# First norm of a decoder layer on one Trainium2 core: fp16 halves split in token layout and turned by DMA transposes

## The chip, the cores and the metric

The kernel runs on one NeuronCore of a Trainium2 chip. The metric is the device time in microseconds (us) of one execution. Engines are named as in the profile: PE is TensorE (PEld its weight loads), DVE is VectorE, ACT is ScalarE, POOL is GpSimd, SP is SyncE, which here only issues DMAs. A name with a q, such as SPq, is the queue of that engine's instructions.

## The reference

One decoder layer over 1024 tokens of 1024 columns, in float32. Cut to what matters:

```python
h = rms_norm(x, norm_mix_pre)                 # x * rsqrt(mean(x*x) + 1e-6) * gain
proj = h @ w_in                               # q, k, v, three conv inputs, two gates
o = stick_breaking_attention(q, k, v)         # 8 heads of 64, strictly causal
m = sigmoid(g_att) * (o @ w_att) + sigmoid(g_conv) * ((cb * causal_dwconv(cc * cx)) @ w_conv)
x = x + rms_norm(m @ w_out, norm_mix_post)
u = causal_dwconv(rms_norm(x, norm_ffn_pre) @ w_up)      # 2 * 2816 columns
a, g = split(u)
x = x + rms_norm((gelu(g) * a) @ w_down, norm_ffn_post)
```

## The kernel before

Every float32 matrix product is made of three fp16 products: an operand is scaled by a power of two and split into a high half (the value rounded to fp16) and a low half (the rest), and high x high, high x low and low x high are summed in PSUM (`PASSES`). The high half is written by an ACT activation, the low half by a DVE `scalar_tensor_tensor`.

This case is about the first stage of `mixer`: the first RMS norm, and the turn of the normed x into `hT`. `hT` is one buffer of shape [128, 2, 8, 1024]: columns of h on the partitions, two halves, eight blocks of 128 columns, 1024 tokens. All products that read h take it from there: the v product has it as the stationary operand (L343, L371), q, k, the conv inputs and the gates as the moving one (L200).

x comes as eight tiles of 128 tokens by 1024 columns, one 512 KB DMA each (`load_x`, L307). The steps of tile tt are small helpers: `square_x` (ACT, sum of squares, L56), `rstd_x` (a DVE step at L170, then a power on POOL at L171), `norm_x` (DVE, times the root and the gain row `gb`, in place, L317), `turn_x` (eight TensorE transposes of float32 blocks into PSUM, L322), `high` (ACT, PSUM to the high half of `hT`, L325), `low` (DVE, PSUM to the low half of `hT`, L328). `gain_max` and `gain_pow2` (DVE, L176 to L186) find the power of two for the halves of h, `s_h`, from the gain row; `high` and `low` use it.

Beside these run the weights of v, four tiles `st[0..3]`: their sums of squares (`sumsq` on ACT for tiles 0, 1, 3; a DVE instruction, `jk_v_2`, L424, for tile 2), their common scale `s_v` (`scale_of`: a few small DVE steps around one tiny matmul with a matrix of ones, L74), their high halves `w_high` (ACT, L375) and low halves `w_low` (DVE, L378). `v_pass(tt, ...)` is a group of v matmuls of token tile tt (L371). `square_w` fetches the raw tile of the next weights (q, then k; DMA at L383) and takes its sum of squares; `open_w` makes its scale (again with a tiny matmul, L74) and its high half (L392), and the function that it returns makes the low half (L396). `v_out` evicts one tile of v (ACT L333, DVE L335). `qk_tile` is a product of q or k, 24 matmuls for each half of the tokens (L200).

The order of this stage is written out by hand: within `tc.manual_schedule(engines={PE, DVE, Activation})` each of these three engines gets its instructions in the order of the program text. SP's queue is not in that set, so that a scheduler places the DMA issues. In the trace each engine starts its instructions in the order of its queue, so one that waits holds up those behind it on its engine. From `v_tile` of tile 4 and the attention on, the order is again the scheduler's.

Of the kernel before, what the change touches and what calls it, by code (L numbers as in the profile page):

```python
# [16 lines left out]
F16 = mybir.dt.float16  # L17
BF16 = mybir.dt.bfloat16
F32 = mybir.dt.float32
I32 = mybir.dt.int32  # L20
AF = mybir.ActivationFunctionType
ALU = mybir.AluOpType
AX = mybir.AxisListType

P = 128
T = 1024
D = 1024
KD = D // P
# [9 lines left out]
class Layer:  # L38
# [225 lines left out]
    def mixer(self, mid):  # L264
        tc, nc, a = self.tc, self.nc, self.a
        hT = self.hp.tile([P, 2, KD, T], F16, tag="hT", name="hT")
        with ExitStack() as ph1:
# [30 lines left out]
                yield  # L298


            with tc.tile_pool(name="ptp", bufs=2, space=bass.MemoryType.PSUM) as ptp:
                gb = self.slot([P, D], F32, "g_pre")
                xt, rt, pt = {}, {}, {}

                def load_x(tt):
                    xt[tt] = self.slot([P, D], F32, f"x{tt}")
                    nc.sync.dma_start(xt[tt], a["x"][ds(tt * P, P), :])  # L307

                def square_x(tt):
                    rt[tt] = self.small(f"r_pre{tt}")  # L310
                    self.sumsq(xt[tt], rt[tt][:, 0:1], f"n_pre{tt}")

                def rstd_x(tt):
                    rt[tt] = self.rstd(rt[tt])

                def norm_x(tt):
                    nc.vector.scalar_tensor_tensor(xt[tt], xt[tt], rt[tt], gb, ALU.mult, ALU.mult)  # L317

                def turn_x(tt):
                    pt[tt] = ptp.tile([P, KD, P], F32, tag="pt", name=f"pt_pre{tt}")  # L320
                    for k in range(KD):
                        nc.tensor.transpose(pt[tt][:, k, :], xt[tt][:, ds(k * P, P)], self.ident)  # L322

                def high(tt):
                    nc.scalar.activation(hT[:, 0, :, ds(tt * P, P)], pt[tt], AF.Copy, scale=s_h)  # L325

                def low(tt):
                    nc.vector.scalar_tensor_tensor(hT[:, 1, :, ds(tt * P, P)], pt[tt], s_h,  # L328
                                                   hT[:, 0, :, ds(tt * P, P)], ALU.mult, ALU.subtract)

                def v_out(tt, pv):
                    pj = pv.rearrange("p (j two d) -> p j two d", two=2, d=64)
                    nc.scalar.activation(v16[tt // 2][:, tt % 2, :, 0:4:3, :], pj, AF.Copy, scale=2.0 ** -15)  # L333
                    for e in range(2):
                        nc.vector.scalar_tensor_tensor(v16[tt // 2][:, tt % 2, :, 1 + e, :], pj[:, :, e, :], 2.0 ** -15,  # L335
                                                       v16[tt // 2][:, tt % 2, :, 3 * e, :], ALU.mult, ALU.subtract)
# [18 lines left out]
                    if i == 0:  # L355
                        load_x(1)
                load_x(2)
                load_x(3)
                nc.sync.dma_start(self.cmw, a["conv_mix"])
                nc.sync.dma_start(self.cfw, a["conv_ffn"])  # L360
                wv = [self.wh.tile([P, 2, D], F16, tag="wh", name=f"wh_v_{i}") for i in range(4)]
                sm_v = self.small("sm_v")
                ET = mybir.EngineType
                pv = [None] * 4

                def v_pass(tt, ks, passes, first=False, last=False):
                    if first:
                        pv[tt] = pm.tile([P, NH], F32, tag="pm", name=f"pv{tt}")
                    todo = [(k, p) for k in ks for p in passes]
                    for n, (k, (hi, wi)) in enumerate(todo):  # L370
                        nc.tensor.matmul(pv[tt], hT[:, hi, k, ds(tt * P, P)], wv[k // 2][:, wi, ds((k % 2) * NH, NH)],  # L371
                                         start=first and n == 0, stop=last and n == len(todo) - 1)
# [4 lines left out]
                def w_low(i):  # L377
                    nc.vector.scalar_tensor_tensor(wv[i][:, 1, :], st[i], s_v, wv[i][:, 0, :], ALU.mult, ALU.subtract)  # L378
# [20 lines left out]
                def square_w(n, which):  # L399
                    raw[which] = fetch(n)  # L400
                    sm0[which] = self.small(f"sm_{which}0")
                    self.sumsq(raw[which], sm0[which][:, 0:1], f"{which}0_0")
# [2 lines left out]
                    for _ in range(n):  # L405
                        next(gen)

                for tt in range(4, 8):
                    load_x(tt)
                with tc.manual_schedule(engines={ET.PE, ET.DVE, ET.Activation}):  # L410
                    square_x(0)
                    rstd_x(0)
                    norm_x(0)
                    turn_x(0)
                    g_sm = self.gain_max(gb, "pre")
                    self.sumsq(st[0], sm_v[:, 0:1], "v_0")
                    square_x(1)
                    s_h, inv_h = self.gain_pow2(g_sm, 2)
                    self.sumsq(st[1], sm_v[:, 1:2], "v_1")
                    rstd_x(1)  # L420
                    norm_x(1)
                    turn_x(1)
                    high(0)
                    nc.vector.scalar_tensor_tensor(self.slot([P, D], F32, "jk_v_2"), st[2], 1.0, st[2], ALU.mult, ALU.mult,  # L424
                                                   accum_out=sm_v[:, 2:3])
                    self.sumsq(st[3], sm_v[:, 3:4], "v_3")
                    high(1)
                    s_v, inv_wv = self.scale_of(sm_v, 4, keep=True)
                    low(0)
                    low(1)  # L430
                    for i in range(4):
                        w_high(i)
                        if i == 2:
                            square_x(2)
                        for tt in range(2):
                            v_pass(tt, (2 * i, 2 * i + 1), ((0, 0), (1, 0)), first=i == 0)
                    w_low(0)
                    rstd_x(2)
                    w_low(1)
                    norm_x(2)  # L440
                    v_pass(0, range(0, 4), ((0, 1),))
                    turn_x(2)
                    square_x(3)
                    rstd_x(3)
                    w_low(2)
                    w_low(3)
                    v_pass(0, range(4, 8), ((0, 1),), last=True)
                    square_x(4)
                    norm_x(3)
                    high(2)  # L450
                    rstd_x(4)
                    square_w(1, "q")
                    low(2)
                    v_pass(1, range(8), ((0, 1),), last=True)
                    turn_x(3)
                    norm_x(4)
                    v_out(0, pv[0])
                    square_w(2, "k")
                    lq = open_w(1, "q")
                    high(3)  # L460
                    low(3)
                    v_out(1, pv[1])
                    square_x(5)
                    v_pass(2, range(8), PASSES, first=True, last=True)
                    rstd_x(5)
                    turn_x(4)
                    lq()
                    lk = open_w(2, "k")
                    norm_x(5)
                    high(4)  # L470
                    v_out(2, pv[2])
                    lk()
                    low(4)
                    square_x(6)
                    rstd_x(6)
                    v_pass(3, range(8), PASSES, first=True, last=True)
                    turn_x(5)
                    high(5)
                    norm_x(6)
                    v_out(3, pv[3])  # L480
                    low(5)
                    self.wdone["v"] = wv, inv_wv
                    self.wpos = self.fpos = 3
                    cst = self.small("cst", keep=True)

                    nc.vector.tensor_scalar(cst[:, 0:1], inv_h, inv_h, 2.0 ** 27, ALU.mult, ALU.mult)
                    nc.vector.tensor_scalar(cst[:, 1:2], inv_h, inv_wv, 2.0 ** 15, ALU.mult, ALU.mult)
                    inv_ov = cst[:, 1:2]
                    gens0 = [qk_tile(0, "q"), qk_tile(0, "k")]
                    run(gens0[0], 8)  # L490
                    square_x(7)
                    rstd_x(7)
                    turn_x(6)
                    high(6)
                    norm_x(7)
                    low(6)
                    self.fetch_to(4)
                    run(gens0[1], 8)
                    turn_x(7)
                    high(7)  # L500
                    low(7)


            pat = pha.enter_context(tc.tile_pool(name="pat", bufs=1, space=bass.MemoryType.PSUM))
# [781 lines left out]
```

## Time and profile before

| | |
|---|---|
| time, median of 3 runs | 1368.22 us (1367.43 to 1368.27) |
| profiled execution, first to last instruction (span) | 1365.7 us; no other time is given for this execution |
| PE busy | 1336.1 us, 98% of the span |
| DVE busy | 1028.6 us, 75% |
| ACT busy | 860.7 us, 63% |
| DMA | 96.06 MB, mean 70 GB/s |
| mean granted TensorE clock | 0.998 |

The profile was taken of one execution. Its page gives the busy time of each engine, the span in 40 slices of 34 us, the DMA queues, and the costliest groups of instructions. The first slice holds the stage of this case. In a row of the timeline the columns are start, duration, engine, line, operation, output and inputs, count, and in brackets the idle time before it with the instruction that ended it; several like instructions in a row are merged and have a count.

### The profile page before, as it was taken

How to read it: one execution, taken by the hardware profiler on the slowest of the kernel's cores; microseconds unless marked ns; L12 is line 12 of the kernel's file. 1: busy time of each engine (PE TensorE's matmuls, PEld its weight loads, DVE VectorE, ACT ScalarE, POOL GpSimd, SP SyncE). 2: the span in 40 equal slices, each digit the busy share in tenths (PEclk: the TensorE clock that was granted, in tenths of full speed). 3: DMA queues.
4: the chain of work that ended last, by engine and by line, in shares of the span. 5: the costliest groups of instructions: out<-in, count | busy, mean ns of one | idle time of the engine just before them, and what ended most of it. 6: DMA issues, size and time to landing. Idle time of an engine off the chain costs nothing. (4 is left out here: it accounts for less than half of the span.)

```text
span 1365.7 us, 16990 instructions
## 1 busy us (share of the span) xinstructions
PE 1336.1 (98%) x6651; PEld 607.7 (44%) x6651; DVE 1028.6 (75%) x1610; ACT 860.7 (63%) x1204; POOL 34.2 (3%) x52
## 2 busy tenths in 40 slices
PE   6999999999999999999999999999999999999997
PEld 3444444444444444444454444444444444444443
DVE  6667777777775965878788985984894896699855
ACT  6668778787775775666466577652761673476524
POOL 2000000000000000000010000000000000000002
PEclk9999999999999999999999999999999999999999
DMA  7102111101111121351331123122220321313216
GB/s 264 62 1 62 32 31 32 38 25 39 40 31 47 32 62 31 93 185 36 119 124 62 62 62 123 39 87 85 70 78 16 123 62 62 109 45 124 63 46 109
DMA packets 26576, 96.06 MB, mean 70 GB/s; under 512 B 3072, under 2 KB 3200, under 8 KB 26496
## 3 DMA queue, kind: packets, MB, share of 16 engines
q1 hardware_dynamic: 25056, 89.74, 20.3%
q0 software_dynamic: 1440, 5.24, 2.1%
q8 instruction: 52, 0.85, 0.2%
q14 instruction: 28, 0.23, 0.1%
HBM read 86.58 MB, written 8.39 MB: 70 GB/s over the span
## 5 line engine op out<-in xcount | busy, mean ns | idle before, releaser
L1156 PEld LDWEIGHTS <-wh_u 128*128 128x128 f16 x1848 | 178.8, 98 | 217.3 <-issue 3.5
L1048 PE MATMUL pd<-wdh,f 128*128 128x512 f16 (+1 forms) x1068 | 230.3, 377 | 2.8 <-ACT wdh L86 1.2
L1048 PEld LDWEIGHTS <-f 128*128 128x128 f16 x1068 | 104.4, 98 | 127.2 <-issue 4.3
L86 ACT ACTIVATE wh_u<-ws_u,sc 128x1024 f16<-128x1024 f32 (+1 forms) x66 | 64.7, 998 | 102.9 <-DVE sc L78 79.3
L1055 DVE SCALAR_TENSOR_TENSOR yacc<-pd,sd,yacc 128x512 f32<-128x512 f32 (+1 forms) x81 | 58.5, 740 | 72.7 <-PE pd L1048 65.2
L1156 PEld LDWEIGHTS <-wh_g 128*128 128x128 f16 x588 | 56.9, 98 | 68.7 <-issue 0.4
L859 PE MATMUL py<-wh_wo,m 128*128 128x512 f16 x384 | 83.9, 379 | 0.0
L87 DVE SCALAR_TENSOR_TENSOR wh_u<-ws_u,sc,wh_u 128x1024 f16<-128x1024 f32 (+1 forms) x66 | 72.1, 1099 | 9.5 <-ACT wh_u L86 9.4
L643 DVE SCALAR_TENSOR_TENSOR w<-zc,w 128x1024 f16<-128x1024 f32 (+3 forms) x48 | 45.7, 955 | 34.5 <-ACT w L642 34.4
L622 ACT ACTIVATE sp<-zc 128x1024 f32<-128x1024 f32 (+3 forms) x48 | 40.2, 838 | 46.7 <-DVE zc L615 29.1
L600 PE MATMUL A<-sh,tri 128*128 128x512 f16 (+3 forms) x352 | 67.8, 322 | 0.0
L1233 DVE SCALAR_TENSOR_TENSOR ugu<-cgu,cw_g,ugu 128x1023 f32<-128x1023 f32 (+1 forms) x44 | 56.2, 1278 | 11.3 <-ACT ugu L1231 10.9
L1233 DVE SCALAR_TENSOR_TENSOR ua<-cau,cw_a,ua 128x1023 f32<-128x1023 f32 (+1 forms) x44 | 56.1, 1276 | 1.4 <-ACT ua L1231 1.3
L859 PEld LDWEIGHTS <-m 128*128 128x128 f16 x384 | 37.5, 98 | 44.1
L626 DVE TENSOR_TENSOR sh<-sp,sh 128x1024 f16<-128x1024 f32 (+3 forms) x48 | 45.7, 952 | 12.9 <-ACT sh L625 12.7
L640 ACT ACTIVATE zc<-zc 128x1024 f32<-128x1024 f32 (+3 forms) x48 | 40.0, 834 | 15.4 <-DVE zc L638 15.0
L638 DVE SCALAR_TENSOR_TENSOR zc<-A,zc 128x1024 f32<-128x1024 f32 (+3 forms) x48 | 45.5, 949 | 2.3 <-PE A L600 2.3
L56 ACT ACTIVATE jk_u<-ws_u 128x1024 bf16<-128x1024 f32 x44 | 46.4, 1054 | 0.9
L200 PE MATMUL pk<-hT,wh_k 128*128 128x512 f16 x192 | 46.8, 380 | 0.0
L200 PE MATMUL pq<-hT,wh_q 128*128 128x512 f16 x192 | 44.3, 379 | 1.3 <-DVE sc L79 1.3
L623 ACT ACTIVATE sp<-sp,one 128x1024 f32<-128x1024 f32 (+3 forms) x48 | 44.6, 928 | 0.8
L200 PE MATMUL pcb<-hT,wh_cb 128*128 128x512 f16 x192 | 44.8, 379 | 0.0
(620 smaller groups left out, 2606.4 us busy)
## 6 DMA issues: line engine op xcount, KB each, us to landing
ws_u<-w_up_nt SPq DMA_DIRECT2D x44, 512.0 KB, 3.7
ds<-w_down SPq DMA_DIRECT2D x22, 512.0 KB, 6.1
wd<-w_down SPq DMA_DIRECT2D x22, 512.0 KB, 3.7
ws_g<-w_in_nt SPq DMA_DIRECT2D x14, 512.0 KB, 3.6
x<-x SPq DMA_DIRECT2D x8, 512.0 KB, 8.0
ws_wo<-w_out SPq DMA_DIRECT2D x8, 512.0 KB, 7.1
xr<-x SPq DMA_DIRECT2D x8, 512.0 KB, 4.3
out<-x SPq DMA_DIRECT2D x7, 512.0 KB, 2.9
```

Of the source, the lines that this page charges most:

```text
L56: self.nc.scalar.activation(self.junk(f"jk_{name}"), src, AF.Square, accum_out=acc)
L86: self.nc.scalar.activation(dst[:, 0, :], src, AF.Copy, scale=s)
L87: self.nc.vector.scalar_tensor_tensor(dst[:, 1, :], src, s, dst[:, 0, :], ALU.mult, ALU.subtract)
L200: nc.tensor.matmul(ps, w[:, wi, ds(k * P, P)], hT[:, hi, k, ds(c * NH, NH)], start=n == 0, stop=n == last)
L600: nc.tensor.matmul(out, w, mv, skip_group_check=True, **kw)
L626: nc.vector.tensor_tensor(sh[:, 1, :, off:], sp[:, :, off:], sh[:, 0, :, off:], ALU.subtract)
L643: nc.vector.scalar_tensor_tensor(w[:, 1, :, off:], zc[:, :, off:], 2.0 ** 14, w[:, 0, :, off:], ALU.mult, ALU.subtract)
L859: nc.tensor.matmul(ps, m16[k][:, hi, ds(tt * P, P)], wo[k][:, wi, sl], start=k == 0 and p == 0, stop=k == 7 and p == 2)
L1048: nc.tensor.matmul(pd[nh], f16[g][k][:, hi, ds(tt * P, P)], w[k][:, wi, ds(*part)], start=run is runs[0] and n == 0, stop=run is runs[-1] ...
L1055: nc.vector.scalar_tensor_tensor(y[:, sl], ps, sm[:, 0:1], y[:, sl], ALU.mult, ALU.add)
L1156: nc.tensor.matmul(ps, w[wt][:, wi, ds(wc * NH + k * P, P)], self.block(i, hi, k), start=first and n == 0, stop=n == 3 * KH - 1, skip_grou ...
L1233: nc.vector.scalar_tensor_tensor(u[:, lag:], c[:, :T - lag], sm[:, 2 - lag:3 - lag], u[:, lag:], ALU.mult, ALU.add)
```

## The change

`turn_x` and the PSUM pool that it wrote go away. `high(tt)` and `low(tt)` now write the halves of the normed x in token layout into a tile `nt` of the pool `o16p` (four buffers of 4 KB a partition, later used by the attention's outputs), and two DMA transposes, issued on SP, each turn one half of 128 x 1024 fp16 (256 KB) into `hT`. The order by hand now also covers SP: the loads of x tiles 3 to 7, of the two conv weight arrays, and the fetches of the q and k weights are issued where they stand in the text, behind the transposes of earlier tiles. The steps of `gain_max` and `gain_pow2` move ahead of `norm_x(0)`, and `high`/`low` of a tile move up in the order, right behind its norm or soon after.

```diff
-            with tc.tile_pool(name="ptp", bufs=2, space=bass.MemoryType.PSUM) as ptp:
+            with ExitStack():
...
-                def turn_x(tt):
-                    pt[tt] = ptp.tile([P, KD, P], F32, tag="pt", name=f"pt_pre{tt}")
-                    for k in range(KD):
-                        nc.tensor.transpose(pt[tt][:, k, :], xt[tt][:, ds(k * P, P)], self.ident)
-
                 def high(tt):
-                    nc.scalar.activation(hT[:, 0, :, ds(tt * P, P)], pt[tt], AF.Copy, scale=s_h)
+                    nt[tt] = self.o16p.tile([P, 2, D], F16, tag="o16", name=f"nt_pre{tt}")
+                    nc.scalar.activation(nt[tt][:, 0], xt[tt], AF.Copy, scale=s_h)
 
                 def low(tt):
-                    nc.vector.scalar_tensor_tensor(hT[:, 1, :, ds(tt * P, P)], pt[tt], s_h,
-                                                   hT[:, 0, :, ds(tt * P, P)], ALU.mult, ALU.subtract)
+                    nc.vector.scalar_tensor_tensor(nt[tt][:, 1], xt[tt], s_h, nt[tt][:, 0], ALU.mult, ALU.subtract)
+                    for hl in range(2):
+                        nc.sync.dma_start_transpose(hT[:, hl, :, ds(tt * P, P)], nt[tt][:, hl])
...
                 load_x(2)
-                load_x(3)
-                nc.sync.dma_start(self.cmw, a["conv_mix"])
-                nc.sync.dma_start(self.cfw, a["conv_ffn"])
...
-                for tt in range(4, 8):
-                    load_x(tt)
-                with tc.manual_schedule(engines={ET.PE, ET.DVE, ET.Activation}):
+                with tc.manual_schedule(engines={ET.PE, ET.DVE, ET.Activation, ET.SP}):
                     square_x(0)
+                    g_sm = self.gain_max(gb, "pre")
                     rstd_x(0)
+                    s_h, inv_h = self.gain_pow2(g_sm, 2)
                     norm_x(0)
-                    turn_x(0)
-                    g_sm = self.gain_max(gb, "pre")
+                    high(0)
                     self.sumsq(st[0], sm_v[:, 0:1], "v_0")
+                    low(0)
+                    load_x(3)
                     square_x(1)
-                    s_h, inv_h = self.gain_pow2(g_sm, 2)
-                    self.sumsq(st[1], sm_v[:, 1:2], "v_1")
                     rstd_x(1)
                     norm_x(1)
-                    turn_x(1)
-                    high(0)
+                    self.sumsq(st[1], sm_v[:, 1:2], "v_1")
+                    high(1)
+                    low(1)
+                    for tt in (4, 5):
+                        load_x(tt)
                     nc.vector.scalar_tensor_tensor(self.slot([P, D], F32, "jk_v_2"), st[2], 1.0, st[2], ALU.mult, ALU.mult,
                                                    accum_out=sm_v[:, 2:3])
                     self.sumsq(st[3], sm_v[:, 3:4], "v_3")
-                    high(1)
                     s_v, inv_wv = self.scale_of(sm_v, 4, keep=True)
-                    low(0)
-                    low(1)
                     for i in range(4):
                         w_high(i)
...
                     norm_x(2)
                     v_pass(0, range(0, 4), ((0, 1),))
-                    turn_x(2)
+                    high(2)
                     square_x(3)
                     rstd_x(3)
                     w_low(2)
                     w_low(3)
+                    low(2)
+                    for tt in (6, 7):
+                        load_x(tt)
+                    nc.sync.dma_start(self.cmw, a["conv_mix"])
+                    nc.sync.dma_start(self.cfw, a["conv_ffn"])
                     v_pass(0, range(4, 8), ((0, 1),), last=True)
                     square_x(4)
                     norm_x(3)
-                    high(2)
+                    high(3)
                     rstd_x(4)
+                    low(3)
                     square_w(1, "q")
-                    low(2)
                     v_pass(1, range(8), ((0, 1),), last=True)
-                    turn_x(3)
                     norm_x(4)
                     v_out(0, pv[0])
+                    high(4)
                     square_w(2, "k")
                     lq = open_w(1, "q")
-                    high(3)
-                    low(3)
+                    low(4)
                     v_out(1, pv[1])
                     square_x(5)
                     v_pass(2, range(8), PASSES, first=True, last=True)
                     rstd_x(5)
-                    turn_x(4)
                     lq()
                     lk = open_w(2, "k")
                     norm_x(5)
-                    high(4)
                     v_out(2, pv[2])
+                    high(5)
                     lk()
-                    low(4)
+                    low(5)
                     square_x(6)
                     rstd_x(6)
                     v_pass(3, range(8), PASSES, first=True, last=True)
-                    turn_x(5)
-                    high(5)
                     norm_x(6)
+                    high(6)
                     v_out(3, pv[3])
-                    low(5)
+                    low(6)
...
                     run(gens0[0], 8)
                     square_x(7)
                     rstd_x(7)
-                    turn_x(6)
-                    high(6)
                     norm_x(7)
-                    low(6)
+                    high(7)
+                    low(7)
                     self.fetch_to(4)
                     run(gens0[1], 8)
-                    turn_x(7)
-                    high(7)
-                    low(7)
```

More of the change, by code (lines that the diff above doesn't have):

```diff
@@ L298, in qk_tile @@
                 yield
-            with tc.tile_pool(name="ptp", bufs=2, space=bass.MemoryType.PSUM) as ptp:
+            with ExitStack():
                 gb = self.slot([P, D], F32, "g_pre")
-                xt, rt, pt = {}, {}, {}
+                xt, rt, nt = {}, {}, {}
                 def load_x(tt):
```

## The prediction

> **What bounds the kernel now.** I read the page first, then the busy time by stretches, then PE's timeline, then the timelines of ACT, DVE and SP in the first 60 us. Of the page:
>
> ```profile
> span 1365.7 us, 16990 instructions
> ...
> PE 1336.1 (98%) x6651; PEld 607.7 (44%) x6651; DVE 1028.6 (75%) x1610; ACT 860.7 (63%) x1204; POOL 34.2 (3%) x52
> ...
> PE   6999999999999999999999999999999999999997
> ```
>
> PE is full from the second slice on. The stretches (length, PE busy, PEld, DVE, ACT, POOL, granted clock, DMA share, GB/s) cut the start at PE's own events:
>
> ```profile
> 0.00:16.74 16.74, 4.10 (x17) 3.38 (x18) 8.59 (x23) 10.23 (x15) 3.45 (x12) 1.00 0.86 333
> 16.74:31.00 14.26, 14.26 (x59) 6.50 (x59) 9.89 (x12) 8.92 (x14) 3.59 (x3) 1.00 0.73 240
> 31.00:58.60 27.60, 25.34 (x140) 13.89 (x139) 18.44 (x45) 18.77 (x30) 2.55 (x3) 1.00 0.12 40
> 58.60:1365.70 1307.10, 1292.41 (x6438) 583.93 (x6437) 991.72 (x1534) 822.79 (x1149) 24.63 (x34) 1.00 0.22 66
> ```
>
> After 58.60 PE works 1292.41 of 1307.10 us, so what the start loses or gains there reaches the end nearly whole. PE's timeline of the start:
>
> ```profile
> 16.74 10.73 PE L371 MATMUL pv<-wh_v,hT 128*128 128x512 f16 x36 [1.95 <-ACT wh_v L375]
> 27.31 1.04 PE L322 MATMUL pt_pre<-ident,x 128*128 128x128 f32 x8
> 28.18 2.75 PE L371 MATMUL pv<-wh_v,hT 128*128 128x512 f16 x12
> 30.77 1.04 PE L322 MATMUL pt_pre<-ident,x 128*128 128x128 f32 x8
> 32.79 0.16 PE L74 MATMUL pr<-rb,ones 128*128 128x1 bf16 x1 [0.98 <-DVE rb L71]
> 32.81 5.34 PE L371 MATMUL pv<-wh_v,hT 128*128 128x512 f16 x24
> 37.99 1.04 PE L322 MATMUL pt_pre<-ident,x 128*128 128x128 f32 x8
> 38.87 0.16 PE L74 MATMUL pr<-rb,ones 128*128 128x1 bf16 x1
> ...
> 56.25 1.04 PE L322 MATMUL pt_pre<-ident,x 128*128 128x128 f32 x8
> 57.12 0.19 PE L74 MATMUL pr<-rb,ones 128*128 128x1 bf16 x2
> 58.60 0.38 PE L200 MATMUL pq<-hT,wh_q 128*128 128x512 f16 x1 [1.29 <-DVE sc L79]
> ```
>
> Three things: the first v matmul starts at 16.74, after the weights' scale; `v_pass(2)` starts at 32.81, after the tiny matmul of q's scale; a turn takes PE 0.87 us (37.99 to 38.87). So the change can win at most six turns in the full stretch, 6 x 0.87 = 5.2 us; the first two turns lie in idle time. Matmuls run at 0.216 us each in the later groups ((5.34 - 0.16)/24), but the first 36 took 10.73.
>
> **The change, part by part: the first matmul.** ACT and DVE rows of before (merged timeline, two engines):
>
> ```profile
> 4.48 1.06 ACT L56 ACTIVATE jk_n_pre<-x 128x1024 bf16<-128x1024 f32 x1 [2.40 <-DMA x<-x]
> ...
> 7.92 1.06 ACT L56 ACTIVATE jk_v<-ws_v 128x1024 bf16<-128x1024 f32 x1 [2.29 <-DMA ws_v<-w_v]
> ...
> 9.19 1.06 ACT L56 ACTIVATE jk_n_pre<-x 128x1024 bf16<-128x1024 f32 x1
> ...
> 13.04 1.06 ACT L56 ACTIVATE jk_v<-ws_v 128x1024 bf16<-128x1024 f32 x1 [0.41 <-DMA ws_v<-w_v]
> ...
> 15.55 3.22 ACT L375 ACTIVATE wh_v<-ws_v,sc 128x1024 f16<-128x1024 f32 x3
> ...
> 5.66 0.15 DVE L170 TENSOR_SCALAR r_pre<-r_pre 128x1 f32<-128x1 f32 x1 [2.45 <-ACT jk_n_pre L56]
> ...
> 6.65 1.29 DVE L317 SCALAR_TENSOR_TENSOR x<-x,r_pre,g_pre 128x1024 f32<-128x1024 f32 x1 [0.83 <-DMA g_pre<-g_mix_pre]
> ...
> 7.85 1.21 DVE L176 TENSOR_REDUCE g_pre<-g_pre 128x1 f32<-128x1024 f32 x1
> ...
> 12.40 1.22 DVE L424 SCALAR_TENSOR_TENSOR jk_v<-ws_v 128x1024 f32<-128x1024 f32 x1
> ...
> 14.22 0.16 DVE L68 TENSOR_REDUCE sc<-sm_v 128x1 f32<-128x4 f32 x1 [0.60 <-ACT jk_v L56]
> ...
> 15.15 2.47 DVE L328 SCALAR_TENSOR_TENSOR hT<-pt_pre,g_pre,hT 128x1024 f16<-128x1024 f32 x2
> ...
> 20.08 1.52 POOL L171 TENSOR_TENSOR r_pre<-r_pre,neghalf 128x1 f32<-128x1 f32 x1 [8.92 <-DVE r_pre L170]
> ```
>
> `gain_max` now stands before the norm on DVE: it starts when the gain row lands, at 6.65, and takes 1.21. The root's two steps follow, about 1.0 us as from 5.66 to 6.65, with the four small gain steps beside them: norm of tile 0 from 8.9 to 10.2. `high(0)` stands on ACT ahead of all the weights' sums, so ACT idles from 5.7 to 10.2, though the first v weights are there at 7.92. From there, with 1.1 for a half on ACT, 1.27 for a square (7.92 to 9.19), 1.25 for a half on DVE: `high(0)` to 11.4; sum of v tile 0 to 12.7; square of x1 to 13.9; norm of x1 from 14.9 to 16.2, beside it the sum of v tile 1; `high(1)` to 17.5; sum of v tile 3 to 18.7. DVE: `low(0)` 11.5 to 12.8, `low(1)` 17.5 to 18.8, `jk_v_2` to 20.1. The scale then takes 1.33 to the first `w_high` (14.22 to 15.55) and 1.19 more to PE (15.55 to 16.74). First matmul: 22.7, **6.0 later**. Here the wait is for the order on ACT and DVE; the two transposes of tile 1 are issued at 17.5 and 18.8 and hide behind it if they land within 3.9 us.
>
> **The transposes themselves.** No row shows one. Nearest rows: the stretch in which the x tiles load, and the DMA issues (KB each, median us from issue to landing):
>
> ```profile
> 10.00:15.00 5.00, 2.13 (x9) 1.81 (x10) 3.06 (x7) 4.10 (x8) 0.55 (x1) 1.00 1.03 403
> ```
>
> ```profile
> x<-x SPq DMA_DIRECT2D x8, 512.0 KB, 8.0
> ...
> ws_q<-w_in_nt SPq DMA_DIRECT2D x4, 512.0 KB, 3.9
> ...
> out<-o SPq DMA_DIRECT2D x2, 256.0 KB, 2.6
> ```
>
> A transpose moves 256 KB. At the 403 GB/s of that stretch it would hold the engines 0.65 us and land in 2.6; as slow as an x tile in the crowd, 8.0. A gain below nothing is excluded: these are added transfers. I take 1 to 2 us held and 2.6 to 3.9 to land, since the store of the same size is the nearest row.
>
> [...]
>
> **The v passes.** PE runs its 36 and 12 matmuls from 22.7 without the turn of tile 2. The last ten need `w_low(2)` and `w_low(3)`. On DVE these stand behind `rstd_x(3)`, and that behind `square_x(3)`, which ACT does only after the new `high(2)`: `w_high` 2 to 24.8, square of x2 to 25.9, root with POOL's 1.52 and norm to 28.9, `high(2)` to 30.1, square of x3 to 31.4, `w_low` 2 and 3 from 31.5 to 34.0. So these passes end at about 36.1 (30.9 before).
>
> **The q weights, the dearest step.** SP now goes by the text: q's fetch stands behind the transposes of tile 3. Before, it was issued at 18.84:
>
> ```profile
> 18.84 0.33 SPq L383 DMA_DIRECT2D ws_q<-w_in_nt  x1
> ...
> 29.39 1.05 ACT L56 ACTIVATE jk_q<-ws_q 128x1024 bf16<-128x1024 f32 x1
> ...
> 30.43 0.59 ACT L333 ACTIVATE v<-pv 128x512 f16<-128x512 f32 x1
> ...
> 31.93 0.75 DVE L335 SCALAR_TENSOR_TENSOR v<-pv,v 128x256 f16<-128x256 f32 x2
> ```
>
> `low(2)` 34.0 to 35.3, norm of x3 to 36.6, `high(3)` to 37.8, `low(3)` to 39.1. Two issues at 0.33 at least, then q at 39.7, landing 3.9 later at 43.6 and, behind the transposes of tile 3 in the DMA queue, up to 44.5. ACT waits for it with `v_out(0)`, `high(4)` and k's sum queued behind; DVE waits for `v_out(0)` with q's scale behind; PE waits for that scale's tiny matmul with `v_pass(2)` behind. From the start of q's square to `v_pass(2)` I count 1.05, 0.59, 0.75 and 0.4 for cast and tiny matmul, 2.8 (3.4 before, where DVE had a norm between). `v_pass(2)` starts at about 46.8, **14.0 later** than 32.81; the 6.0 above are within these 14.0. PE idles 10.7 us before it.
>
> **PE's pace after a long idle.** The first 36 matmuls took 10.57 where 36 x 0.216 is 7.8: 2.8 us more, though the granted clock stands at 1.00 in that row. After the idle of 0.98 at 32.79 nothing of this shows. An idle of 10.7 is nearer the first case: **+2.8**, between 0 and 2.8. [...]
>
> **What is won.** Behind `v_pass(2)` four turns go, 4 x 0.87 = **-3.5**; those of tiles 2 and 3 fall into idle time that has grown. Tiles 4 to 7 are covered: by the same steps `low(7)` ends at 71.8 and its transposes land by 75.5, while PE is in q and k until 70.4 (46.8 + 96 x 0.216 + 2.8), and then has the v product of tile 4 (24 x 0.216 = 5.2 us), which needs only tile 4. If that cover fails, up to 5 us. The idle of 1.29 at 58.60 may go or stay: -0.6.
>
> Sum: 14.0 + 2.8 - 3.5 - 0.6 = 12.7, and 1365.7 + 12.7 = 1378.4 for the span. The median of the runs lies 2.5 above the span: **1381**. Own range 1373 (no slow pace, a shorter q wait, 3 us for another order of the scheduler behind 58.60) to 1386 (cover of tile 7 lost).
>
> **The rivals.** *The transposes are a queue.* If one holds the DMA engines 4 us, between the rows of 2.6 and 8.0, the loads before them end at 14.3 (the v tile used at 13.04, one more at 1.3), then tile 0's pair to 22.3, x3, tile 1's pair to 31.6, x4 and x5, tile 2's pair to 42.2, x6 and x7, tile 3's pair to 52.8, q to 54.1, `v_pass(2)` at 57.3: 10.5 later than in my sum, 1391.5. With 8.0 the same chain gives q at 86 and the last transposes at 151, against PE work that before ended at 74 (58.60 + three v products of 5.2): 1440 or more. It decides from about 2 us on. For it: the direction of the transfers is new; against it: 256 KB is little. A transfer that is cut into single elements, so not a turn in one piece at all, belongs to this tail. *Faster.* The q fetch does not wait behind tile 3, as SP's order stays the scheduler's, and ACT's late sums cost less than the turns: 1365.7 - 5.2 + 2.5 = 1363. It needs all added waits below 5.2 us, and the first matmul alone takes 6.0. *No slow pace:* 1378, inside my range. *Nothing moves,* gains and waits cancel: 1368.
>
> **How the numbers follow.** My sum has 0.66; the queue 0.26, of which 0.16 up to 4.9 us a transpose (1398, at about 6 us for each further us) and 0.10 beyond; faster 0.05; no change 0.03. The range 1372 to 1398 leaves out the 0.08 and the 0.10. A difference of 0.2% is 2.7 us, what can be told here from no change. Faster 0.05, same 0.03, slower 0.92.
>
> **What would show it.** Right: first matmul near 22.7; q's DMA issued near 39.7, with its square on ACT ended by that DMA; PE idle of about 11 us before `v_pass(2)`, ended through DVE's cast; then a dozen matmuls at double length. Wrong: q issued before tile 3's transposes; transposes that land in over 5 us, or an SP that is held by them; PE idle before q's second half, ended by a transpose.

## The result, and the profile after

| | before | after |
|---|---|---|
| time, median (lowest to highest) | 1368.24 us (1367.43 to 1369.01) | 1386.67 us (1385.81 to 1386.92) |
| span of the profiled execution | 1365.7 us | 1385.2 us |
| ratio after / before, 95% interval | | 1.0133 (1.0119 to 1.0147) |

The change costs 18.4 us in the medians and 19.5 in the spans; 1381 was forecast. The page of the kernel after:

```profile
span 1385.2 us, 16893 instructions
...
PE 1332.9 (96%) x6587; PEld 599.2 (43%) x6587; DVE 1031.8 (74%) x1610; ACT 861.6 (62%) x1204; POOL 34.2 (2%) x52
...
PE   3689999999999999999999999999999999999998
...
PEclk9889999999999999999999999999999999999999
```

PE has 64 matmuls fewer (the eight turns) and 3.2 us less busy time, but 52.3 us idle in place of 29.6. The loss stands in the first three slices, and there the granted clock falls too. The stretches of the kernel after, cut at PE's own events (length; then busy us and count of PE, PEld, DVE, ACT, POOL; granted clock, DMA share, GB/s):

```profile
0.00:21.23 21.23, 0.17 (x2) 0.20 (x2) 9.64 (x24) 10.31 (x15) 3.44 (x12) 1.00 0.92 276
21.23:34.40 13.17, 12.62 (x48) 5.21 (x48) 8.64 (x9) 7.44 (x10) 3.04 (x2) 1.00 0.28 93
34.40:46.90 12.50, 0.19 (x3) 0.03 (x2) 3.54 (x7) 3.71 (x5) 0.55 (x1) 0.69 0.87 237
46.90:70.55 23.65, 23.65 (x98) 10.04 (x97) 15.04 (x30) 11.82 (x18) 2.57 (x3) 0.87 0.35 68
70.55:79.46 8.91, 5.07 (x35) 2.05 (x35) 4.34 (x9) 5.67 (x11) 0.00 (x0) 0.65 0.97 294
79.46:94.00 14.54, 14.54 (x69) 6.67 (x69) 8.41 (x21) 13.36 (x22) 0.00 (x0) 0.86 0.23 74
94.00:441.40 347.40, 347.14 (x1957) 149.13 (x1956) 250.14 (x375) 263.20 (x343) 0.00 (x0) 1.00 0.11 34
441.40:1385.20 943.80, 929.55 (x4384) 425.84 (x4382) 732.04 (x1139) 546.09 (x784) 24.58 (x34) 1.00 0.25 77
```

Two stretches are nearly empty or half empty, 34.40 to 46.90 and 70.55 to 79.46, and each is followed by one with the clock below 1.00. From 94.00 on PE is full. PE's timeline shows both places; below it SP's and ACT's timelines show what they wait for:

```profile
21.23 10.46 PE L365 MATMUL pv<-wh_v,hT 128*128 128x512 f16 x38 [1.62 <-ACT wh_v L369]
32.24 2.32 PE L365 MATMUL pv<-wh_v,hT 128*128 128x512 f16 x10 [0.55 <-DVE wh_v L372]
46.87 0.16 PE L74 MATMUL pr<-rb,ones 128*128 128x1 bf16 x1 [12.31 <-DVE rb L71]
46.90 8.25 PE L365 MATMUL pv<-wh_v,hT 128*128 128x512 f16 x24
...
65.37 5.34 PE L200 MATMUL pk<-hT,wh_k 128*128 128x512 f16 x24
71.40 0.28 PE L591 MATMUL z<-q,k 64*128 64x128 f16 x4 [0.69 <-ACT k L290]
...
79.36 0.16 PE L74 MATMUL pr<-rb,ones 128*128 128x1 bf16 x1 [0.53 <-DVE rb L71]
79.46 4.75 PE L200 MATMUL pq<-hT,wh_q 128*128 128x512 f16 x12
```

```profile
36.80 3.29 SPq L326 DMA_TRANSPOSE hT<-nt_pre  x2
40.14 0.58 SPq L377 DMA_DIRECT2D ws_q<-w_in_nt  x1
...
47.03 25.18 SPq L326 DMA_TRANSPOSE hT<-nt_pre  x8
72.26 0.57 SPq L103 DMA_DIRECT2D ws_q<-w_in_nt  x1
72.88 0.42 SPq L103 DMA_DIRECT2D ws_k<-w_in_nt  x1
```

```profile
44.34 1.06 ACT L56 ACTIVATE jk_q<-ws_q 128x1024 bf16<-128x1024 f32 x1 [8.57 <-DMA ws_q<-w_in_nt]
...
76.32 1.06 ACT L56 ACTIVATE jk_q<-ws_q 128x1024 bf16<-128x1024 f32 x1 [1.41 <-DMA ws_q<-w_in_nt]
```

First place: q's raw tile is fetched at 40.14, behind the transposes of tile 3; its square on ACT starts after a wait of 8.57 that this DMA ends, and PE idles 12.31 before `v_pass(2)`. Second place: the fetches of the next q and k weights (`ws_q`, `ws_k` at L103; q1 and k1 below; before, L103's first fetch was issued at 24.24) stand behind the eight transposes of tiles 4 to 7, which wait for their halves; SP comes to these fetches at 72.26. So q1's square is at 76.32 instead of 52.28, and the second half of q0 starts at 79.46, behind the scale matmuls of q1 and k1 in PE's queue.

After 441.40, where the product with the conv branch's weights begins (`pywc`), the rest takes 943.8 us, against 944.4 before. The first matmul of `pywc` is at 421.3 before and 441.4 after, so the whole loss of 20.1 lies ahead of it. I use this start as a **landmark** for every kernel below: it is free of the scatter of what comes later, but each landmark is read from one profiled execution.

### The profile page after: what moved, and what is told of

The parts are those of the page before. It is cut to its first block, busy times and chain, and to the rows that moved or that the text cites. A ratio compares the mean times of both kernels' runs of the same rounds, so it can differ in the third digit from the quotient of the medians.

```text
span 1385.2 us, 16893 instructions
## 1 busy us (share of the span) xinstructions
PE 1332.9 (96%) x6587; PEld 599.2 (43%) x6587; DVE 1031.8 (74%) x1610; ACT 861.6 (62%) x1204; POOL 34.2 (2%) x52
## 5 line engine op out<-in xcount | busy, mean ns | idle before, releaser
L1224 DVE SCALAR_TENSOR_TENSOR ugu<-cgu,cw_g,ugu 128x1023 f32<-128x1023 f32 (+1 forms) x44 | 56.2, 1277 | 11.3 <-ACT ugu L1222 10.9
L200 PE MATMUL pq<-hT,wh_q 128*128 128x512 f16 x192 | 47.7, 392 | 0.0
L616 ACT ACTIVATE sh<-sp 128x1024 f16<-128x1024 f32 (+3 forms) x48 | 40.1, 835 | 9.7 <-PE A L591 9.1
L200 PE MATMUL pcc<-hT,wh_cc 128*128 128x512 f16 x192 | 45.6, 379 | 0.0
```

What stands on the lines that cost most here:

```text
L200: nc.tensor.matmul(ps, w[:, wi, ds(k * P, P)], hT[:, hi, k, ds(c * NH, NH)], start=n == 0, stop=n == last)
L1224: nc.vector.scalar_tensor_tensor(u[:, lag:], c[:, :T - lag], sm[:, 2 - lag:3 - lag], u[:, lag:], ALU.mult, ALU.add)
```

## The experiments

Landmarks and medians of all of them (minus is earlier than before; "before" ran on the same chip each time):

| kernel | landmark, us against 421.3 | median, before | ratio (95%) |
|---|---|---|---|
| after | +20.1 | 1386.67, 1368.24 | 1.0133 (1.0119 to 1.0147) |
| copies | +18.6 | 1386.04, 1368.55 | 1.0132 (1.0117 to 1.0147) |
| q_early | +11.3 | 1380.51, 1368.55 | 1.0090 (1.0075 to 1.0106) |
| q1k1_early | +18.0 | 1384.79, 1368.55 | 1.0121 (1.0104 to 1.0138) |
| warm | +20.1 | 1387.82, 1368.55 | 1.0143 (1.0128 to 1.0158) |
| before_q_late | +7.0 | 1375.54, 1368.72 | 1.0052 (1.0037 to 1.0067) |
| start_order | +16.8 | 1385.07, 1368.72 | 1.0121 (1.0105 to 1.0138) |
| both_early | +7.3 | 1379.61, 1368.72 | 1.0079 (1.0064 to 1.0094) |
| sp_free | +5.9 | 1375.87, 1368.72 | 1.0055 (1.0040 to 1.0070) |
| all_early | +6.4 | 1374.69, 1367.41 | 1.0041 (1.0027 to 1.0055) |
| best | +0.2 | 1368.69, 1367.41 | 1.0008 (0.9999 to 1.0017) |
| best2 | +4.9 | 1372.95, 1368.96 | 1.0039 (1.0025 to 1.0053) |
| best3 | -2.0 | 1368.08, 1368.22 | 1.0000 (0.9991 to 1.0009) |

Landmark and median do not always move together, and the traces show one reason. Seven of the fourteen kernels' traces have one drop of the granted clock behind the landmark, to a mean of about 0.83 over 10 us, which costs 1.7: q_early, q1k1_early, start_order, sp_free and all_early some 310 us behind it, where PE waits 1.79 for ACT's `hB`, both_early and best3 some 380 us behind it. All fourteen have waits of PE at both places, and where no drop is named the clock stays at 0.99 or above.

My theory A: the loss is the place of the weight fetches in SP's order, plus PE's half pace after the idle (granted clock 0.50 from 46.90 to 52.81); the turn by DMA itself is hidden. Rival B: the transposes, by what they hold or how late they land, set the time.

**Are the transposes slow? (copies)**

```diff
-    nc.sync.dma_start_transpose(hT[:, hl, :, ds(tt * P, P)], nt[tt][:, hl])
+    nc.sync.dma_start(hT[:, hl, :, ds(tt * P, P)], nt[tt][:, hl].rearrange("p (k t) -> p k t", k=KD))
```

> The changed kernel with each DMA transpose replaced by a plain DMA of the same 256 KB in pieces of 256 bytes between the same buffers and at the same place in SP's queue; hT then holds h not turned. Theory A: the order holds everything as before, within 2 us of 1386.7. Rival B (the transposes hold SP or the DMA engines longer than plain transfers do, and that sets the time): 5 us or more are won, 1381 or less.

The transposes in the profile of after (ns of SP's queue held: lowest, median, highest; then us to landing), then the copies in that of copies, with q's fetch and `v_pass(2)` there:

```profile
L326 SPq DMA_TRANSPOSE hT<-nt_pre x16: 1231/1245/1759, 11.0 to 70.9; - x16
...
DMA to landing us min/median/max: 3.0/3.1/4.5
```

```profile
L326 SPq DMA_DIRECT2D hT<-nt_pre x16: 593/596/696, 11.0 to 70.4; - x16
...
DMA to landing us min/median/max: 2.9/2.9/5.7
...
37.76 2.49 SPq L377 DMA_DIRECT2D ws_q<-w_in_nt  x1
...
46.70 7.90 PE L365 MATMUL pv<-wh_v,hT 128*128 128x512 f16 x24
```

The median is the same within the intervals, so B falls as far as it says that a transpose is slower than a copy: a turn of 256 KB lands like a copy of 256 KB in pieces of 256 bytes, in 3.1 us against 2.9. That the traffic of the turns as such sets the time is not excluded by this run, but by q_early and sp_free below, which keep all sixteen transposes. A transpose does hold SP's queue twice as long, 1.25 us against 0.60, but that is not what keeps q late: in copies SP comes to q's fetch 2.4 us earlier, at 37.76, is held by it for 2.49, and `v_pass(2)` starts only 0.2 earlier. From 34.40 to 46.90 the DMA share is 0.87 in after: x tiles 6 and 7, the conv weights and the transposes of tile 3 are on the DMA engines ahead of q. Of the 1.5 us in the landmark, 0.4 are there when the second half of q0 starts (79.06); the rest comes behind it, where copies has a granted clock of 0.98 over the next 4.6 us and after 0.56.

**Is it the place of the first fetches? (q_early, and before_q_late on the kernel before)** In q_early the first fetches of q and k stand behind `low` of the weights, ahead of the transposes of tiles 2 and 3. In before_q_late the kernel before gets its q fetch held back by a one-column DVE copy out of x2, behind `low(2)`.

```diff
                     w_low(0)
+                    raw["q"] = fetch(1)
                     rstd_x(2)
                     w_low(1)
+                    raw["k"] = fetch(2)
```

```diff
-                    square_w(1, "q")
                     low(2)
+                    raw["q"] = self.ws.tile([P, D], F32, tag="ws", name="ws_q0_0")
+                    nc.vector.tensor_copy(raw["q"][:, 0:1], xt[2][:, 0:1])
+                    nc.sync.dma_start(raw["q"], self.wseq[1][1][0])
+                    square_w(1, "q")
```

> The changed kernel with one thing moved: the fetches of the q and k weights are issued behind w_low(0) and w_low(1), ahead of the transposes of tile 2. Theory A (waits of the order by hand): q has landed long before ACT comes to it, its square follows high(3) at about 36, and v_pass(2) starts near 39.3 instead of 46.9, so 7.6 us are won, and up to 2.9 more if PE does not fall to the slow pace in the shorter idle: 1376 to 1379. Rival B (the transposes' own time): v_pass(2) then waits for the transposes instead and less than 3 us is won: 1384 or more.

> The kernel before (TensorE transposes, no transposing DMA) with one wait added: q's fetch waits for a one-column DVE copy behind low(2), so that it is issued at about 31 instead of 18.84. Theory A: q lands at 35, v_pass(2) starts 3.4 us later at 38.2 instead of 32.81, 5.4 us are lost, and 2.8 more if PE falls to the slow pace in an idle of 7 us: 1373.6 to 1376.5. Rival: q's place does not set the time, other waits take over and less than 2 us is lost: below 1370.

PE's timeline of q_early, then of before_q_late:

```profile
39.02 7.03 PE L365 MATMUL pv<-wh_v,hT 128*128 128x512 f16 x24
...
68.42 0.16 PE L74 MATMUL pr<-rb,ones 128*128 128x1 bf16 x1 [2.07 <-DVE rb L71]
```

```profile
36.97 0.16 PE L74 MATMUL pr<-rb,ones 128*128 128x1 bf16 x1 [5.25 <-DVE rb L71]
36.99 8.17 PE L371 MATMUL pv<-wh_v,hT 128*128 128x512 f16 x24
```

q_early wins 6.2 us of median and 8.8 of landmark: `v_pass(2)` starts 7.9 earlier and loses 1.7 instead of 2.9 to the slow pace. The landmark's gain is what A forecast (7.6 to 10.5). The median lies 1.5 above A's range; the profiled execution loses 2.0 behind the landmark (945.8 us from there against 943.8), mostly in the drop of the clock named above. The second place is not mended: q1 is still fetched behind ten transposes, at 63.15, and PE's idle there is 5.5 us against 3.8. before_q_late shows the same mechanism without any transpose: q later, 4.2 us later start (36.99 against 32.81) and 2.8 of slow pace, 7.0 together, which is its landmark; the median is in A's range.

**Is it the second fetches? (q1k1_early, both_early)** The fetches of q1 and k1 move ahead: behind k's first fetch in q1k1_early, behind `low(2)` in both_early, which also has q_early's edit; where these tiles used to be fetched, the one at hand is taken.

```diff
+                    for n in (3, 4):
+                        self.pre[self.wseq[n][0]] = fetch(n)
```

> The changed kernel with the weight tiles of the next pair (q1, k1) fetched behind k0's, ahead of the transposes of tiles 4 to 7, where they now stand behind those of tile 7. Theory A: the second idle of PE (3.84 us between 70.55 and 79.46, and the slow pace after it, 2 to 2.5 us) comes from their scales, which PE has queued ahead of the second half of q0; 3 to 6 us are won: 1381 to 1384. Rival B: the second half of q0 waits for tile 7's transposes anyway (issued at 70.9, landing 3.1 later), and nothing changes: 1386 to 1387.

> The changed kernel with all four fetches moved: q and k behind w_low(0) and w_low(1), q1 and k1 behind the transposes of tile 2. Theory A: the gains of the two single moves add, 7.6 to 10.5 for q and 3 to 6 for q1 and k1: 1370 to 1376. Rival B: above 1380.

Alone, it wins 2.1 at the landmark. The long wait behind 70.55 is gone, but q's fetch is issued 0.8 later, at 40.91 (the two transposes ahead of it hold SP for 4.07 instead of 3.29; why is not shown), and the wait before `v_pass(2)` is 12.98 instead of 12.31; the median alone, between the two expectations, decides nothing. Together with q_early the landmark moves by 12.8, more than the two apart (8.8 and 2.1). In the median, 1379.61, it misses A's range, as does its fastest execution, and most of the landmark's gain over q_early does not come back there. The profiled execution, 1377.13 at a mean granted clock of 0.996, is the fastest of the four; the other three had 0.993 to 0.994 and took 1379.45 to 1380.03. So the 2.5 us between that execution and the median go with a lower clock; where it fell in the other three isn't seen, as they left no trace.

**Is the slow pace the clock, and does work keep it up? (warm)** 52 matmuls whose result nobody reads fill the idle stretch.

```diff
                     v_pass(1, range(8), ((0, 1),), last=True)
+                    pd = dmy.tile([P, NH], F32, tag="d", name="dummy")
+                    for n in range(52):
+                        nc.tensor.matmul(pd, hT[:, 0, n % 8, ds(0, P)], wv[0][:, 0, ds(0, NH)], start=n == 0, stop=n == 51)
```

> The changed kernel with 52 more matmuls of 128x512, whose result is not used, in PE's idle ahead of q's scale (11.2 us of work in 12.3 us of idle). If the slow pace behind that idle is the clock after an idle PE, v_pass(2) takes 5.34 instead of 8.25 and the time falls by 2.9, to about 1383.8. If the slow pace has another cause (the operands, the DMA traffic), it stays at 1386.7 or rises.

PE's timeline and the stretches of warm, both around the end of the dummies:

```profile
34.42 11.39 PE L455 MATMUL dummy<-wh_v,hT 128*128 128x512 f16 x52
47.79 0.16 PE L74 MATMUL pr<-rb,ones 128*128 128x1 bf16 x1 [1.98 <-DVE rb L71]
47.81 7.03 PE L365 MATMUL pv<-wh_v,hT 128*128 128x512 f16 x24
```

```profile
46.00:48.00 2.00, 0.21 (x2) 0.12 (x2) 0.83 (x4) 2.00 (x5) 0.00 (x0) 1.00 0.00 0
48.00:52.00 4.00, 4.00 (x12) 1.50 (x11) 2.77 (x8) 3.52 (x6) 0.15 (x1) 0.57 0.65 125
```

A miss, and an informative one. The dummies ended 1.98 us too early; the granted clock was 0.57 over the next 4 us, and `v_pass(2)` took 7.03, 1.7 too long. It is better than 8.25, but `v_pass(2)` itself started 0.9 later, and the landmark shows no gain. That the slow pace goes with the granted clock is shown (24 matmuls in 7.03 at 0.57 over 4 us, in 5.34 at 1.00 in sp_free); that one can bridge such a gap cheaply is not. Nor does an idle of this length always cost: in best, described below, PE idles 2.38 and then runs at full pace:

```profile
41.16 0.18 PE L74 MATMUL pr<-rb,ones 128*128 128x1 bf16 x1 [2.38 <-DVE rb L71]
41.20 5.34 PE L368 MATMUL pv<-wh_v,hT 128*128 128x512 f16 x24
```

**Is it all of SP's order? (sp_free)**

```diff
-                with tc.manual_schedule(engines={ET.PE, ET.DVE, ET.Activation, ET.SP}):
+                with tc.manual_schedule(engines={ET.PE, ET.DVE, ET.Activation}):
```

> The changed kernel with SP left to the scheduler, as in the kernel before; nothing else is edited. Theory A: the scheduler puts the fetches of q, k, q1 and k1 ahead of the transposes that wait, and the time falls as in the kernels with early fetches, to 1370 to 1380. Rival B: the transposes set the time and SP's order does not matter: 1385 or more.

SP's and PE's timelines of sp_free:

```profile
22.63 0.33 SPq L377 DMA_DIRECT2D ws_q<-w_in_nt  x1
...
31.13 0.33 SPq L103 DMA_DIRECT2D ws_q<-w_in_nt  x1
...
39.17 0.16 PE L74 MATMUL pr<-rb,ones 128*128 128x1 bf16 x1 [1.94 <-DVE rb L71]
39.20 5.34 PE L365 MATMUL pv<-wh_v,hT 128*128 128x512 f16 x24
```

One word of the change taken back wins 10.8 us of its 18.4 (1386.67 to 1375.87; 14.2 of the landmark's 20.1), inside A's range. The scheduler puts q's fetch at 22.63 and q1's at 31.13, between the transposes. It also moves loads of x and the conv weights ahead, so this is the worth of SP's order as a whole. The idle is 1.94, and here `v_pass(2)` runs at full pace, 5.34.

**What is the rest? (start_order, all_early, best, best2, best3)** start_order puts the sum of v tile 0 ahead of `high(0)` and those of tiles 1 and 3 ahead of `high(1)` on ACT, and `jk_v_2` and the scale ahead of `low(1)` on DVE; all_early joins it with both_early; best also reorders tiles 2 to 7, so that squares and sums on which PE waits stand ahead of halves that are not yet due. best2 lets v's scale go ahead of the norm of x1, and the tail's sums ahead of the norm of x7; best3 has best2's start, best's tail and the v product of tile 4 written into PE's order behind the first half of k0. The core of each:

```diff
# start_order
-                    high(0)
                     self.sumsq(st[0], sm_v[:, 0:1], "v_0")
+                    high(0)
# best
-                    rstd_x(3)
                     w_low(2)
...
-                    square_x(4)
+                    rstd_x(3)
                     norm_x(3)
+                    square_w(1, "q")
                     high(3)
+                    square_x(4)
# best3
                     run(gens0[1], 8)
+                    v4 = v_tile(4)
+                    run(v4, 8)
```

> The changed kernel with another order ahead of the first matmul only: ACT takes the sum of v tile 0 before high(0), the sums of v tiles 1 and 3 before high(1), and DVE takes jk_v_2 and the scale before low(1). Theory A: first matmul at about 17.8 instead of 21.23; the steps up to q's fetch follow it, so 2 to 3.4 us are won: 1383 to 1385. Rival: the start is hidden behind the late q fetch, and nothing changes: 1386 to 1387.

> The changed kernel with the four early fetches and the other start order together. Theory A: v_pass(2) at about 36 instead of 39.1 with the early fetches alone, so 3 us less than those: 1374 to 1377. Rival: the tile-2 steps behind the first matmul hold v_pass(2) where it was, 1379 to 1380.

> As all_early, and the order of tiles 2 to 7 written so that nothing waits for something far: DVE takes w_low(2), w_low(3) and low(2) before rstd_x(3); ACT takes q's sum before high(3); q's scale comes right behind v_pass(1); v_out(2) and v_out(3) come behind the halves of the next tile. Theory A: PE goes from the first matmul at 17.7 without a long idle, v_pass(2) at 32 to 33.5, the first half of k0 ends at 53 to 54.5 against 57.1 in the kernel before, and the turns that TensorE no longer makes count: 1363 to 1367, against 1368.5 before. Rival B: the transposes of tiles 4 to 7 land after 60 and PE waits for them: 1368 or more.

> The version of the run before with three more edits of the order: the scale of v's weights ahead of norm_x(1) and all first passes of token tile 0 ahead of those of tile 1 (first matmul about 1.1 us earlier, no wait for tile 1's transposes); v_out(1) and k's scale ahead of high(4), so that the 2.4 us of idle before v_pass(3) goes; the sums of q1 and k1 ahead of v_out(3). Theory A: 2.4 + 1 to 2 us less than 1368.7, so 1364 to 1366, and below the kernel before. Rival B: the transposes of tiles 4 to 7, one after the other behind their halves, hold the second half of q0 at 58 to 59 as before, and the time stays at 1367 to 1369.

> The version best2 with the tail of best (tile 7's square and root ahead of v_out(3), its norm right behind; the sums of q1 and k1 last) and with the v product of token tile 4 written into the order of PE right behind the first half of k0, so that PE has 5.2 us of work while tile 7's transposes land. Theory A: the first half of k0 ends at 54.7, v of tile 4 at 60, when tile 7 has landed; the kernel before is there at 64.1: 1363 to 1366, below the kernel before. Rival B: the chain of DVE steps and transposes of tiles 4 to 7 ends later than 60 and PE waits again: 1367 or more.

start_order starts the first matmul 3.6 earlier, at 17.64, and 3.3 of it reach the landmark, as A forecast: q's fetch moves along, to 36.59. Only 1.6 reach the median, and its trace has one of the drops behind the landmark. all_early comes out inside its range, at 1374.69, but in part by luck: `v_pass(2)` starts 3.4 earlier than in both_early, as forecast, yet after an idle of 3.47 it takes 8.08 instead of 7.03, and the landmark is only 0.9 better. best gives the rest back almost whole: first matmul 17.78, first half of k0 at its end by 56.7 (57.12 before), landmark +0.2; its median, 1368.69, is 1.7 above A's range. best2 is a miss: the start is better (16.61), but with the sums ahead of it the norm of tile 7 is late and four waits of 0.73 to 1.93 follow behind 55. best3 repairs that and is 2.0 ahead at the landmark, of the 5.2 us of turns in the full stretch that could be won at most. Most of the other 3.2 is in its waits on PE (engine, line, what ends them; total us, times, longest):

```profile
PE pv L368 <- DMA hT<-nt_pre: 3.8, 4, 2.3
```

That is 3.8 us of waits which the kernel before didn't have, all of them ahead of or early in `v_pass(2)` and `v_pass(3)`; in return its own waits of 0.98 and 1.29 are gone. From the first matmul to the landmark PE's idle grows from 2.27 to 4.70, by 2.4. Once SP's order no longer hides it, the turn by DMA does stand on PE's path, and takes back nearly half of what the removed turns had freed.

So the median, 1368.08, is in B's range, and even the 2.0 are gone in the end, span 1366.5 against 1365.7. One part is shown: the stretches of best3 behind two waits of 1.04 and 0.85 near 800. The kernel before has them too (1.01 and 0.75), and in its profiled execution the clock stays at 1.00:

```profile
800.00:804.00 4.00, 2.96 (x14) 1.24 (x13) 4.00 (x7) 1.87 (x4) 0.00 (x0) 1.00 0.36 133
804.00:811.00 7.00, 6.15 (x22) 2.39 (x21) 7.00 (x9) 3.50 (x4) 0.00 (x0) 0.76 0.54 151
```

The drop costs 7 x (1 - 0.76) = 1.7 us. The other executions left no trace, but their mean clocks differ in both kernels; that such drops come in some and not in others is my estimate from these clocks. In the runs of this comparison both have executions at a mean clock of 0.999 (best3: four, mean 1366.5; before: eight, mean 1366.9) and at 0.997 (four, 1368.3; eight, 1369.1). At equal clock best3 is 0.4 to 0.8 ahead, less than can be told. No version here beats the kernel before by more than the intervals.

## Why the prediction was right, and where it was not

The forecast was 1381 in a range of 1372 to 1398; 1386.67 is slower, as said, and 5.7 above the point. It is 0.7 outside the range that the sum itself gave (1373 to 1386), and inside the wide one only because that leaves room for slow transposes, which did not come: that part is luck. Step by step:

- **First matmul:** 21.23 against a forecast 22.7. `high(0)` ran at 9.79 instead of 10.2, and the chain from there to PE took 11.4 instead of 12.5. The gain went on down the chain: `low(3)` ended at 37.08 instead of 39.1. It was lost in the next step.
- **q's fetch behind tile 3, the dearest step:** right in the mechanism, and the numbers agree in part by luck. Issue 40.14 (39.7), `v_pass(2)` at 46.90 (46.8), its cause as forecast; the idle was 12.31 (10.7), as the passes before it ended earlier. But the chain came to the two transposes 2.0 earlier than in the sum, and they held SP for 3.29 where the sum had 0.66; the two errors cancel. (With half that hold, in copies, `v_pass(2)` starts only 0.2 earlier.) q_early and before_q_late show the late fetch as the cause, from both sides.
- **Slow pace after the idle:** +2.8 forecast, an estimate from the first matmuls (10.57 against 7.8); 8.25 - 5.34 = 2.9 measured, and here the granted clock shows it: 0.87 over the stretch from 46.90.
- **Four turns, -3.5:** right: the first half of k0 ended at 70.55 (70.4). Up to here the shift against before is 70.55 - 57.12 = 13.4.
- **The cover by the v product of tile 4, and -0.6 for the idle at 58.60:** wrong; this is the mis-sized term. From 70.55 to the landmark the shift grows by 20.1 - 13.4 = 6.7, where I had -0.6. I followed q's fetch past the transposes, but not the next two fetches, of q1 and k1, past those of tiles 4 to 7. Their scale matmuls stand in PE's queue ahead of q0's second half, and the scheduler had put the attention's first products there, not v of tile 4. Idle grew by 3.84 - 1.29 = 2.55; the rest is nearly all pace: from the end of that half of k0 to the landmark PE is busy 366.76 us with 2058 matmuls, against 362.89 with 2059 before, at a clock of 0.50 in the second half of that hole and 0.56 over the next 4.6 us. I had the fallen cover in the range ("up to 5 us"), with another cause, the late transposes of tile 7; those were in time. q1k1_early and both_early remove the long wait, and all they win at the landmark, 2.1 alone and 4.0 behind q_early, lies in this term; the remainder isn't split further.
- **The transposes:** 3.1 to landing, inside the forecast 2.6 to 3.9. The DMA engines were held 1.4, inside 1 to 2: the first transpose of tile 2 has them alone from 28.60 to 33.00, at a share of 0.31 (4.40 x 0.31). SP's queue was held 1.25 by each, where the sum had 0.33. So of the signs of being wrong one came, SP is held; but the condition of the rival, 4 us of the DMA engines for each transpose, did not, and the idle before q0's second half ends through DVE's cast of a scale, not with a transpose. The plain copies of the same size landed in 2.9.
- **Nothing won:** the 5.2 us of turns in the full stretch were the most that could come. best3, with another order and tile 4's v product in the order by hand, is 2.0 ahead at the landmark.

## What to carry to other kernels

When a transfer that waits for computed data is put on a queue that issues in order, list every later DMA on that queue, not only the next: each now waits for that data, as q's fetch did, issued at 40.14 behind the transposes of tile 3, and here loads of weights that had been issued 20 to 48 us earlier became the critical path. A stall on PE is to be counted with the slow pace that can follow it, here 1.7 to 2.9 us behind some idles from 1.79 up to 12.98, and nothing behind others of up to 2.43. And work that lay in PE's idle time anyway, as the first turns did, wins nothing when it is removed.

## What the runs showed of the hardware

- In after the granted clock is 0.50 from 39.16 to 52.81, 13.65 us, from inside the idle of 12.31 into `v_pass(2)`, and from 73.30 to 83.53, 10.23 us, from inside the second hole to behind it, where no single wait in that hole is longer than 0.91; it is 1.00 between the two and up to 100. In warm it is 0.57 over the 4.00 us behind the idle of 1.98, an estimated 3.4 us at half (2 x 0.43 x 4.00). The three lengths are about four, three and one times 3.4.
- The length of an idle does not decide alone whether the clock falls. Behind an idle of 1.98 `v_pass(2)` took 7.03, 1.7 too long (warm), while idles of 1.94 (sp_free) and 2.35 to 2.43 (best3, best, best2) cost nothing; the same wait of 1.79, for ACT's `hB`, left the clock at 1.00 in before, and in q_early a drop that costs 1.7 stands there.
- One kernel's executions spread with their mean clock: the kernel before takes a mean of 1366.9 us at a mean clock of 0.999, and 1369.1 at 0.997.
- In the first matmuls the profile gives a clock of 1.00, though they run slower than like ones later: 36 of 128x512 took 10.57 us in before, against 7.8 at the later pace. The clock records of that trace begin at 22.44, so the 1.00 ahead of it is not a reading.
